# Reciprocal roots of the second layer's key-head sums by Newton steps on VectorE, and another order of that layer's weight units

## The chip, the cores and the metric

The kernel runs on one core of a Trainium2 chip. TensorE (PE in the profile) multiplies matrices, VectorE (DVE) and ScalarE (ACT) work element by element, GpSimd (POOL) does small things and starts the accumulating DMAs, SyncE (SP) starts the other DMAs. The engines have a queue each, which they work through in order; semaphores tie them together. The metric is the device time of one execution in microseconds, with the median over some executions.

## The reference

Two decoder layers on 512 tokens of width 1024, in float32. Each layer normalises, makes one wide projection, feeds four head groups from it, gates each group, and projects back onto the residual stream:

```python
h = rmsnorm(x, norm_g)
p = h @ W_in                        # 3488 columns, cut up among the groups
# A: latent attention (MLA), 4 heads, key = 64 plain + 32 rotary columns
# B: short gated convolution   C: chunked causal gMLP   D: MoBA, 4 heads, blocks of 256 keys
y = concat(A * silu(ga), B * silu(gb), C * silu(gc), D * silu(gd))
x = x + y @ W_out

def rmsnorm(x, g):
    y = x * lax.rsqrt(jnp.mean(x * x, axis=-1, keepdims=True) + EPS)
    return y * g
```

Queries and keys of the head groups are normalised per head as well. For four heads and 512 tokens, the sums of one kind (rs_q, rs_k for MLA, rs_mq, rs_mk for MoBA) fill a tile of 128 partitions x 16: four token tiles by four heads. The reciprocal root of such a tile is what is changed here.

## The kernel before, in words

A float32 product is made of three matmuls: each operand is split in a high part (rounded, whi, hTh, yTh) and a low part (the rest, wlo, hTl, yTl), and high x high, low x high and high x low are summed in PSUM. A weight unit (up to 128 x 1024) is loaded by SP into one of two raw buffers (NRAW), then `split_units` makes the high part by a copy on ACT or DVE, and `low_half` the low part by a subtraction on DVE, which frees the raw buffer for a later load.

In the second layer, the products are formed with sums of token parts and of weights. Units named p11 ... p22 and e11 ... e22 belong to the two big products so formed, ga, gb, gd and cb are the columns of gates and of the convolution; each has parts 0 and 1, which are units of their own. The unit names are cut in the profile: raw_p, whi_p, wlo_p for p.., px, py, pz for their results in PSUM, ex, ey, ez for those of e... Sums of weights are made by DMA: SP copies one operand, and then a DMA of POOL adds the other (t and in_w_o_dram in the rows).

No engine's order is written by hand. While the program is built, a planner (`Order`, `Chain`, `Slots`) keeps a clock for every engine and a cost for every instruction, and emits each instruction when its time has come. `main` walks the units in the order of a list, for the second layer `SEQ1`, and issues their matmuls whenever nothing of higher priority is due; the heads, norms and splits are chains that run beside it. So a change of the list or of one rule of splitting moves instructions on all engines, also far from the place. FAR is such a rule: a unit at least FAR units ahead of the one that PE is at is split in one instruction of 1024 columns instead of two of 512, if its index is over a bound.

The keys K of the second layer go through: squares and sums on ACT and DVE (`head_means`), eps added on DVE and the power on POOL (`head_rstd`, tile rs_k), two multiplications of K by rs_k on DVE (`key_scale`, 128x512 each), then transposes on PE (t1a; t0a is the same for Q), whose copies hi1a, lo1a, hi0a, lo0a enter the scores sa. The scores of head after head follow, first those of MLA (sa, pa, pTa, oa), and then those of MoBA (mq0d, mq1d, mk0d, mk1d, sd, pd, pTd, od), with products of units between them. zz is the high part of an operand of a later e product, yD what MoBA gives to the output projection (oz, ox, oy).

In the rows L190 is the helper that emits on ACT, DVE and POOL, L220 the one for PE and L384 the one for DMA.

Of the kernel before, what the change touches and what calls it, by code (L numbers as in the profile page):

```python
# [13 lines left out]
I32 = mybir.dt.int32  # L14
AF = mybir.ActivationFunctionType
ALU = mybir.AluOpType
AX = mybir.AxisListType

P = 128
S = 512  # L20
NT = S // P
D = 1024
# [27 lines left out]
EFEAT = ((2, 6), (10, 12))  # L50
TSE = 26000.0
SSUMS = {"p3": 0, "p2": 1, "p1": 2, "p22": 3}
SEQ1 = ['p11', 'p21', 'p3', 'p4', 'ga0', 'p2', 'p1', 'p22', 'ga1', 'e11', 'e21', 'e3', 'e4', 'e2', 'e1', 'cb0', 'e22', 'gb0', 'gd0', 'cb1', 'gb1', 'gd1']
K0, K1, KK = (2, 3, 0, 1), (4, 5, 6, 7), (0, 2, 3, 1)
ZPROD = ("b11", "t3", "b21", "t4", "t2", "t1", "b22")
TS0 = 58000.0
FAR = 3
DLO = ()
LZ = (True, False)
MLAGO = 'p4'  # L60
TZ1 = 270000.0
DLAND = 6000.0
SGLOAD = 'p3'
TAIL = ((0, 256), (256, 512))
# [106 lines left out]
def free_size(ap):  # L171
    n = 1
    for d in ap.shape[1:]:
        n *= d
    return n


class Chain:
# [26 lines left out]
        return self._emit("G", 290 + 2.0 * free_size(a[0]), f, a, k)  # L205

    def pow(self, f, *a, **k):
        return self._emit("G", 400 + 165 * free_size(a[0]), f, a, k)

    def pe(self, cost, f, *a, **k):  # L210
        if self.t != self.pe_t:
# [21 lines left out]
def hybrid_trunk(ctx: ExitStack, tc: tile.TileContext, x, positions, norm_g, w_c, w_f, w_t, w_o, mla_q_norm_g,  # L233
# [3 lines left out]
    V, A, G, PE = nc.vector, nc.scalar, nc.gpsimd, nc.tensor  # L237
# [16 lines left out]
    o = Order()  # L254
# [5 lines left out]
    t2S = Slots(o, NT2, lambda name, dt=F32: t2p.tile([P, S], dt, tag="t2", name=name))  # L260
# [43 lines left out]
    def dma(ch, nbytes, dst, src):  # L304

        o.clk["D"] = max(o.clk["D"], ch.t) + nbytes / 360.0
        move(nc.sync, dst, src)
        ch.t = o.clk["D"] + 2000.0

    x1d = dr.tile([S, D], F32, name="x1d")  # L310

# [36 lines left out]
    def add_unit(*a):  # L348
        u = Unit(*a)
        units[u.name] = u  # L350
        u.idx = len(order)
        order.append(u)
# [28 lines left out]
    def move(q, dst, src, **k):  # L381

        if len(src.shape) < 4:
            q.dma_start(dst, src, **k)  # L384
            return
        for g in range(2):
            q.dma_start(dst[:, 2 * g:2 * g + 2], src[:, g], **k)
# [11 lines left out]
    def t_sums(*streams):  # L399

        gap = 4000.0 if len(streams) == 1 else 3000.0
        for i in range(3):
            steps = []
            for l, src, t, b in streams:
                for n, x, y in (((f"{t}1", f"{b}11", f"{b}12"), (f"{t}3", f"{b}12", f"{b}22")),
                                ((f"{t}2", f"{t}1", f"{b}22"),), ((f"{t}4", f"{t}2", f"{b}21"),))[i]:
                    steps += [(l, src, n, x, y, j) for j in range(2)]
            for l, src, n, x, _, j in steps:
                o.clk["D"] = max(o.clk["D"], o.now) + 1500.0
                move(nc.sync, src(l, n, j), src(l, x, j))  # L410
                yield o.now + gap
            yield o.now + gap
            for l, src, n, _, y, j in steps:
                o.clk["G"] = max(o.clk["G"], o.now) + 1000.0
                move(nc.gpsimd, src(l, n, j), src(l, y, j), accum_op=ALU.add, max_dma_last_dim=1024)
                o.set(tsum_ev[l, n, j], o.now + 10000.0)
                yield o.now + gap
            yield o.now + (8000.0 if len(streams) == 1 else 0.0)
# [6 lines left out]
    for l in range(DEPTH):  # L425
# [3 lines left out]
        add_unit(mla_w_ukv[l], 1, 512, f"ukv_{l}")  # L429
        for n in SEQ1 if l in STOK else SEQ:  # L430
            if n in SPROD:
# [57 lines left out]
    def split_units(i0, i1):  # L489
        for u in order[i0:i1]:  # L490
            ch = Chain(o)
            if u.name != "c0_0":
                yield from ch.wait(u.loaded)
            u.hi, u.lo = yield from u.slots.get(ch, u.name)
            if u.name[:-2] in DLO:
                yield from dma_split(u, ch)
                continue
            n = u.a * u.b
            gain = {"uq": 2 * int(u.name[-1]), "ukv": 4 + int(u.name[-1])}.get(u.name[:-2])
            if gain is not None:  # L500
                yield from ch.wait(pc_ev)
            whole = False
            for i in range(2):
                if whole:
                    break
                if u.name == "c0_0":
                    yield from ch.wait(u.landed[i])
                while ch.t > o.now + SLACK:
                    yield ch.t - SLACK
                while not u.wanted and max(o.clk["A"], o.clk["V"]) > o.now + WSLACK:  # L510
                    yield o.now + 100.0
                whole = i == 0 and gain is None and u.idx >= at[0] + FAR and u.idx > 5
                c2 = Chain(o, max(o.now, ch.t))
                hi, lo, raw = (z[:, :n] if whole else u.part(z, i) for z in (u.hi, u.lo, u.raw))
                g = None
                if gain is not None:
                    c = gain + (i if u.a == 2 else 0)
                    g = pcol[:, c:c + 1]
                if o.clk["V"] + 900.0 < o.clk["A"] and u.idx > 3 or u.idx == 0 and i == 0:
                    if g is None:  # L520
                        yield from c2.dve_fast(V.tensor_copy, hi, raw)
                    else:
                        yield from c2.dve(V.tensor_scalar, hi, raw, g, None, op0=ALU.mult)
                else:
                    yield from c2.act(A.activation, hi, raw, AF.Copy, scale=1.0 if g is None else g)
                for j in range(2) if whole else (i,):
                    o.set(u.high[j], c2.t)
                o.spawn(low_half(u, i, c2, lo, raw, hi, g, whole), None, LOPRIO if u.idx < 4 else 5)
                ch.t = max(ch.t, c2.t - LAT)

    def dma_split(u, ch):

        while ch.t > o.now + SLACK:
            yield ch.t - SLACK
        while not u.wanted and max(o.clk["A"], o.clk["V"]) > o.now + WSLACK:
            yield o.now + 100.0
        ch.t = max(ch.t, o.now)
        yield from ch.act(A.activation, u.hi, u.raw, AF.Copy)
        for e in u.high:
            o.set(e, ch.t)  # L540
        yield from ch.act(A.activation, u.lo, u.hi.bitcast(F32), AF.Copy, scale=-1.0)
        u.raw_slots.put(ch)

        def add():
            while ch.t > o.now:
                yield ch.t
            o.clk["G"] = max(o.clk["G"], o.now) + 1000.0
            move(nc.gpsimd, four(u.lo) if u.name[:-3] in EPROD else u.lo, u.src, accum_op=ALU.add, max_dma_last_dim=1024)
            for e in (*u.half, u.ready):
                o.set(e, o.now + DLAND)  # L550
        o.spawn(add(), None, 4)

    def low_half(u, i, ch, lo, raw, hi, g, whole):
        while o.clk["V"] > o.now + VSLACK and u.idx > at[0] + URGENT:
            yield o.now + 100.0
        ch.t = max(ch.t, o.now)
        if g is None:
            yield from ch.dve(V.tensor_tensor, lo, raw, hi.bitcast(F32), op=ALU.subtract)
        else:
            yield from ch.dve(V.scalar_tensor_tensor, lo, in0=raw, scalar=g, in1=hi.bitcast(F32),  # L560
                              op0=ALU.mult, op1=ALU.subtract)
        o.set(u.half[i], ch.t)
        if whole:
            o.set(u.half[1], ch.t)
        if u.half[1 - i].t is not None:
            ch.t = max(ch.t, u.half[1 - i].t)
            u.raw_slots.put(ch)
            o.set(u.ready, ch.t)
# [10 lines left out]
    at = [0]  # L579
# [12 lines left out]
    nhalf = cst.tile([P, 4], F32, name="nhalf")  # L592
# [167 lines left out]
    for l in range(DEPTH):  # L760
        L = Layer()
# [255 lines left out]
    def head_means(ch, L, n, t, z):  # L1017
# [11 lines left out]
        yield from ch.dve(V.tensor_reduce, L.rs[n][:, t, :], sq, axis=AX.X, op=ALU.add)  # L1029
        t2S.put(ch)  # L1030

    def head_rstd(ch, L, n, eps):

        r = L.rs[n]
        if isinstance(eps, float):
            yield from ch.dve(V.tensor_scalar, r, r, 1.0, eps, op0=ALU.mult, op1=ALU.add)
        else:
            yield from ch.dve(V.tensor_tensor, r, r, eps.unsqueeze(2).to_broadcast([P, NT, 4]), op=ALU.add)
        r2 = r.rearrange("p t h -> p (t h)")
        yield from ch.pow(G.tensor_tensor, r2, r2, nhalf[:, 0:1].to_broadcast([P, 4 * NT]), op=ALU.pow)  # L1040
        o.set(L.rs_ev[n], ch.t)

    def key_scale(ch, L, n, K):
# [100 lines left out]
    def kv_chain(L, t, kv_ps, t0):  # L1144
# [25 lines left out]
        for i in range(NT):  # L1170
            yield from ch.wait(L.stat[i])
        yield from head_rstd(ch, L, "k", L.e2[:, :, 1])
        yield from key_scale(ch, L, "k", K[:, :, :, 0:64])
        o.set(L.kd, ch.t)
# [712 lines left out]
    def main():  # L1887
# [223 lines left out]
        for L in layers:  # L2111
# [21 lines left out]
            st, st2 = ({"bank": {}, "ev": {}, "f32": {}} for _ in range(2))  # L2133
            for n in SEQ1 if L.stok else SEQ:
                if n in EPROD:
# [133 lines left out]
    for l in STOK:  # L2269
        o.spawn(t_sums((l, z_src, "t", "b")), TZ1, 4)  # L2270
    o.spawn(start())
# [51 lines left out]
```

## Time and profile before

| what | value |
|---|---|
| median of 3 runs | 504.42 us (503.38 to 504.62) |
| profiled execution | 502.23 us, its span 500.5 us |
| mean granted clock of TensorE | 0.992 |
| PE busy | 480.7 us, 96% of the span |
| DVE, ACT, POOL busy | 398.2, 343.8, 137.1 us (80%, 69%, 27%) |

The first layer lasts until about 250 us, the second from there to the end. The span is the profiled time from the first to the last instruction; 1.7 us of the execution lie around it. Idle time of an engine stands in the rows in brackets, with the engine and tile that ended it. An engine that is busy 96% of the span sets the time except in its gaps.

### The profile page before, as it was taken

The numbers are of one execution on the slowest core, as the hardware profiler recorded it, in microseconds if no ns is written. First come the engines' busy times: TensorE is split into PE (matmuls) and PEld (weight loads), VectorE is DVE, ScalarE is ACT, GpSimd is POOL, SyncE is SP. The second block draws the span as 40 slices with busy tenths as digits, with TensorE's granted clock in tenths as the row PEclk, the third lists the DMA queues.
The fourth block names the chain that finished last, engine by engine and source line by source line (L and its number), as shares of the span: only waits on it lengthen the run. The fifth ranks groups of instructions, "written<-read, shape, count | busy, mean of one in ns | idle before, by whom it ended". The sixth has DMA issues, their size and how long they took to land.

```text
span 500.5 us, 7430 instructions
## 1 busy us (share of the span) xinstructions
PE 480.7 (96%) x2416; PEld 406.8 (81%) x2416; DVE 398.2 (80%) x781; ACT 343.8 (69%) x891; POOL 137.1 (27%) x201
## 2 busy tenths in 40 slices
PE   8999999999989999999999995999999979999996
PEld 7888888888878888888899874887888768888875
DVE  4697686677897887789896687797997789988982
ACT  5897856786457874365676888498985657986540
POOL 8839583601521052000120139060302200000000
PEclk9999999999999999999999999899999989999999
DMA  8856889999599697875762368683755844675762
GB/s 272 282 152 213 187 233 316 258 239 273 125 342 225 216 282 174 309 288 181 230 204 79 126 229 272 151 169 126 185 151 207 177 144 174 203 230 173 294 208 85
DMA packets 50271, 104.95 MB, mean 210 GB/s; under 512 B 6118, under 2 KB 31032, under 8 KB 49784
## 3 DMA queue, kind: packets, MB, share of 16 engines
q1 hardware_dynamic: 32656, 87.30, 50.3%
q0 software_dynamic: 17472, 17.10, 22.3%
q8 instruction: 19, 0.31, 0.2%
q14 instruction: 20, 0.16, 0.1%
q10 hardware_dynamic: 104, 0.07, 0.1%
HBM read 96.33 MB, written 41.68 MB: 276 GB/s over the span
## 4 chain that ended last, share of the span: by engine, by line
PE 78%; DMA 7%; DVE 5%; ACT 4%; issue 2%; POOL 2%; SPq 1%; DVEq 0%; POOLq 0%; ACTq 0%
PE oy L220 6%; PE kv L220 5%; PE cq L220 5%; PE oz L220 4%; PE sq L220 4%; PE ox L220 4%; PE ga L220 4%; PE gb L220 4%; PE gd L220 4%; PE cb L220 4%; PE py L220 3%; PE sa L220 3%; PE ez L220 2%; PE ex L220 2%; PE gc L220 2%
## 5 line engine op out<-in xcount | busy, mean ns | idle before, releaser
L190 ACT ACTIVATE pd<-pd,mnd 128x512 f32<-128x512 f32 (+3 forms) x58 | 30.6, 558 | 5.3 <-DVE mnd L190 5.2
L190 ACT ACTIVATE pa<-pa,mna 128x512 f32<-128x512 f32 (+3 forms) x56 | 29.2, 553 | 2.3 <-DVE mna L190 2.0
L384 POOL DMA_DIRECT2D t<-in_w_o_dram x16 | 20.3, 1346 | 28.6 <-DMA t<-t 27.9
L190 ACT ACTIVATE phd<-pTd 128x512 fp32r<-128x512 f32 (+1 forms) x24 | 12.6, 524 | 14.1 <-PE pTd L220 13.9
L190 ACT ACTIVATE whi_t<-raw_t 128x1024 fp32r<-128x1024 f32 x16 | 16.7, 1051 | 7.4 <-DMA raw_t<-t 7.3
L220 PE MATMUL cq<-whi_c,hTh 128*128 128x416 f32 x64 | 20.7, 368 | 0.8 <-ACT hTh L190 0.7
L190 ACT ACTIVATE pha<-pTa 128x512 fp32r<-128x512 f32 (+1 forms) x24 | 12.6, 527 | 12.6 <-PE pTa L220 12.5
L220 PE MATMUL cq<-whi_c,hTl 128*128 128x416 f32 x64 | 19.8, 356 | 1.0 <-DVE hTl L190 1.0
L190 DVE CUSTOM_DVE_ANT_0 pd<-sd,maskb,rs_mq 128x512 f32<-128x512 f32 (+3 forms) x32 | 16.7, 546 | 4.5 <-PE pTd L220 3.0
L220 PE MATMUL cq<-wlo_c,hTh 128*128 128x416 f32 x64 | 20.0, 358 | 0.0
L190 DVE CUSTOM_DVE_ANT_0 pa<-sa,maskb,rs_q 128x512 f32<-128x512 f32 (+3 forms) x32 | 16.4, 542 | 3.5 <-ACT junk L190 2.6
L190 DVE TENSOR_TENSOR wlo_t<-raw_t,whi_t 128x1024 fp32r<-128x1024 f32 x16 | 19.1, 1214 | 0.0
L190 DVE TENSOR_TENSOR wlo_p<-raw_p,whi_p 128x1024 fp32r<-128x1024 f32 (+1 forms) x18 | 18.1, 1016 | 0.0
L190 DVE TENSOR_TENSOR wlo_e<-raw_e,whi_e 128x512 fp32r<-128x512 f32 (+1 forms) x19 | 17.7, 936 | 0.3 <-ACT whi_e L190 0.2
L190 DVE TENSOR_TENSOR pla<-pTa,pha 128x512 fp32r<-128x512 f32 (+1 forms) x24 | 14.3, 596 | 4.2 <-ACT pha L190 4.1
L190 POOL TENSOR_SCALAR xss<-xss 128x1 f32<-128x1 f32 x4 | 2.5, 633 | 54.4 <-ACT jk L190 48.4
L190 ACT ACTIVATE whi_p<-raw_p 128x1024 fp32r<-128x1024 f32 (+1 forms) x14 | 11.9, 870 | 7.7 <-PE ga L220 4.0
L190 ACT ACTIVATE whi_e<-raw_e 128x512 fp32r<-128x512 f32 (+1 forms) x16 | 12.7, 812 | 5.2 <-DMA raw_e<-in_w_f_dram 4.7
L190 ACT ACTIVATE whi_b<-raw_b 128x1024 fp32r<-128x1024 f32 x12 | 12.6, 1056 | 5.3 <-DMA raw_b<-in_w_o_dram 5.2
L190 POOL TENSOR_TENSOR ms<-ms,nhalf 128x2 f32<-128x2 f32 x8 | 7.5, 943 | 31.4 <-DVE ms L190 23.4
L190 DVE TENSOR_TENSOR pld<-pTd,phd 128x512 fp32r<-128x512 f32 (+1 forms) x24 | 14.0, 596 | 2.3 <-ACT phd L190 2.2
L220 PE MATMUL pTd<-ident,pd 128*128 128x128 f32 x80 | 12.7, 273 | 3.2 <-ACT zz L190 3.1
(546 smaller groups left out, 1882.2 us busy)
## 6 DMA issues: line engine op xcount, KB each, us to landing
t<-in_w_o_dram POOLq DMA_DIRECT2D x16, 512.0 KB, 9.8
raw_t<-t SPq DMA_DIRECT2D x16, 512.0 KB, 4.5
raw_b<-in_w_o_dram SPq DMA_DIRECT2D x12, 512.0 KB, 4.5
t<-in_w_o_dram SPq DMA_DIRECT2D x8, 512.0 KB, 5.8
p<-in_w_t_dram POOLq DMA_DIRECT2D x8, 512.0 KB, 14.9
t<-t SPq DMA_DIRECT2D x8, 512.0 KB, 4.9
raw_p<-p SPq DMA_DIRECT2D x8, 512.0 KB, 4.1
raw_e<-e SPq DMA_DIRECT2D x8, 512.0 KB, 3.3
```

The lines of the kernel that those rows point to most:

```text
L190: f(*a, **k)
L220: f(*a, **k)
L384: q.dma_start(dst, src, **k)
```

## The change

The reciprocal root of rs_k in the second layer (only this one of the eight) is made by a first guess from the float's bits and three Newton steps: ten DVE instructions on 128x16, in a work tile named newton, where one power on POOL stood. In `SEQ1`, p2 stands ahead of ga0, ga1 ahead of p22, and gd0 behind cb1. FAR is 2 instead of 3, and the bound on the index is 10 instead of 5; this rule holds for both layers. POWC and DLAT are names for numbers that were there before, with the same values.

```diff
-SEQ1 = ['p11', 'p21', 'p3', 'p4', 'ga0', 'p2', 'p1', 'p22', 'ga1', 'e11', 'e21', 'e3', 'e4', 'e2', 'e1', 'cb0', 'e22', 'gb0', 'gd0', 'cb1', 'gb1', 'gd1']
+SEQ1 = ['p11', 'p21', 'p3', 'p4', 'p2', 'ga0', 'p1', 'ga1', 'p22', 'e11', 'e21', 'e3', 'e4', 'e2', 'e1', 'cb0', 'e22', 'gb0', 'cb1', 'gd0', 'gb1', 'gd1']
...
-FAR = 3
+FAR = 2
...
+NEWT = ("k",)
+POWC = 165
+DLAT = 2000.0
...
-                whole = i == 0 and gain is None and u.idx >= at[0] + FAR and u.idx > 5
+                whole = i == 0 and gain is None and u.idx >= at[0] + FAR and u.idx > 10
...
+    def newton_rstd(ch, r):
+
+        m = free_size(r)
+        tab = yield from t2S.get(ch, "newton")
+        y, z = tab[:, :m], tab[:, m:2 * m]
+        yield from ch.dve(V.tensor_scalar, y.bitcast(I32), r.bitcast(I32), -0.5, 1597463007.0, op0=ALU.mult, op1=ALU.add)
+        for i in range(3):
+            yield from ch.dve(V.tensor_tensor, z, y, y, op=ALU.mult)
+            yield from ch.dve(V.scalar_tensor_tensor, z, in0=z, scalar=-0.5, in1=r, op0=ALU.mult, op1=ALU.mult)
+            yield from ch.dve(V.scalar_tensor_tensor, r if i == 2 else y, in0=z, scalar=1.5, in1=y, op0=ALU.add, op1=ALU.mult)
+        t2S.put(ch)
+
     def head_rstd(ch, L, n, eps):
...
-        yield from ch.pow(G.tensor_tensor, r2, r2, nhalf[:, 0:1].to_broadcast([P, 4 * NT]), op=ALU.pow)
+        if L.l == 1 and n in NEWT:
+            yield from newton_rstd(ch, r2)
+        else:
+            yield from ch.pow(G.tensor_tensor, r2, r2, nhalf[:, 0:1].to_broadcast([P, 4 * NT]), op=ALU.pow)
         o.set(L.rs_ev[n], ch.t)
```

What this does to the engines' rows can only be seen in the program that the planner gives. PE has the same 2236 rows, DVE 792 instead of 775, ACT 614 instead of 636, POOL 166 instead of 169; the order changes in both layers.

On PE in the second layer, the transposes of Q and K for the first two MLA heads (t0a, t1a) before the change, nine matmuls of ga behind the last matmul of px:

```order
L220 MATMUL ga_1_3468<-hTh_1_2820,whi_ga_1_3341 128x512
L220 MATMUL ga_1_3468<-hTl_1_2821,whi_ga_1_3341 128x512
L220 MATMUL ga_1_3468<-hTh_1_2820,wlo_ga_1_3342 128x512
L220 MATMUL t0a_3482<-ident,Q_3032 96x128 x4
L220 MATMUL t1a_3483<-ident,K_3033 96x128 x4
L220 MATMUL ga_1_3468<-hTh_1_2820,whi_ga_1_3341 128x512
```

And now:

```order
L223 MATMUL py_1_3501<-whi_p_1_3459,yTh 128x512
L223 MATMUL py_1_3501<-wlo_p_1_3460,yTh 128x512
L223 MATMUL py_1_3501<-whi_p_1_3459,yTl 128x512
L223 MATMUL t0a_3618<-ident,Q_3040 96x128 x4
L223 MATMUL t1a_3619<-ident,K_3041 96x128 x4
L223 MATMUL py_1_3501<-whi_p_1_3488,yTh 128x512
```

They have moved 57 matmuls back: between px and t0a stand now 24 of py (unit p2), 24 of ga0 and 18 of py (unit p1). Behind t1a come 6 more of p1, 24 of ga1 and 6 of p22 ahead of the next scores sa.

On DVE, from the addition of eps to rs_k to the second multiplication of K; before:

```order
L190 TENSOR_TENSOR rs_k<-rs_k,e_2355 128x16
L190 TENSOR_TENSOR rbq_3364<-Q_3032,sinT 128x16x16
L190 TENSOR_TENSOR wlo_ga_1_3342<-raw_ga_1_3293,whi_ga_1_3341 128x1024
L190 TENSOR_TENSOR Q_3032<-Q_3032,cosT 128x16x32
L190 TENSOR_TENSOR yTl<-a_2931,yTh 128x4x128
L190 TENSOR_TENSOR yTl<-a_3013,yTh 128x4x128
L190 TENSOR_TENSOR Q_3032<-Q_3032,rbq_3364 128x16x32
L190 TENSOR_TENSOR wlo_p_1_3397<-raw_p_1_3352,whi_p_1_3396 128x1024
L190 TENSOR_TENSOR K_3033<-K_3033,rs_k 128x8x64
```

Now the first rows of the same stretch:

```order
L193 TENSOR_TENSOR rs_k<-rs_k,e_2345 128x16
L193 TENSOR_TENSOR rbq_3387<-Q_3040,sinT 128x16x16
L193 TENSOR_SCALAR newton<-rs_k 128x16
L193 TENSOR_TENSOR newton<-newton 128x16
L193 TENSOR_TENSOR rbq_3387<-Q_3040,sinT 128x16x16
L193 TENSOR_TENSOR wlo_p_1_3343<-raw_p_1_3299,whi_p_1_3342 128x1024
L193 SCALAR_TENSOR_TENSOR newton<-newton,rs_k 128x16
L193 TENSOR_TENSOR Q_3040<-Q_3040,cosT 128x16x32
```

The ten steps stand one by one among the other work, the last of them in row 495 (the eps is row 460), and the two multiplications of K in rows 499 and 506; before they were 8 and 12 rows behind the eps.

On ACT, where the MoBA heads of the second layer begin (mq1d and mk0d are operands of the first scores sd, whi_e and whi_cb the high parts of units of e and of cb0); before:

```order
L190 ACTIVATE mq0d_4289<-tmqd_4274 64x512
L190 ACTIVATE mk0d_4299<-tmkd_4275,pcol 64x512
L190 ACTIVATE whi_e_1_4277<-raw_e_1_4246 128x1024
L190 ACTIVATE mq1d_4302<-tmqd_4274 64x512
L190 ACTIVATE mk0d_4299<-tmkd_4275,pcol 64x512
```

And now:

```order
L193 ACTIVATE mq0d_4350<-tmqd_4344 64x512
L193 ACTIVATE mk0d_4360<-tmkd_4345,pcol 64x512
L193 ACTIVATE whi_cb_1_4311<-raw_cb_1_4306 128x1024
L193 ACTIVATE whi_e_1_4366<-raw_e_1_4309 128x1024
L193 ACTIVATE mq1d_4364<-tmqd_4344 64x512
L193 ACTIVATE mk0d_4360<-tmkd_4345,pcol 64x512
```

The whi_e in the new rows is that of unit e22 (part 0), which stood before behind the exponentials pd of the first MoBA head, directly ahead of the copy zz. On POOL, the first of the two accumulating DMAs that follow stands now ahead of a memset of kl1d, which waited for the first heads; before, both stood behind it.

More of the change, by code (lines that the diff above doesn't have):

```diff
@@ L207, in pow @@
     def pow(self, f, *a, **k):
-        return self._emit("G", 400 + 165 * free_size(a[0]), f, a, k)
+        return self._emit("G", 400 + POWC * free_size(a[0]), f, a, k)
     def pe(self, cost, f, *a, **k):
@@ L307, in dma @@
         move(nc.sync, dst, src)
-        ch.t = o.clk["D"] + 2000.0
+        ch.t = o.clk["D"] + (DLAT if o.now > 40000.0 else 2000.0)
     x1d = dr.tile([S, D], F32, name="x1d")
```

## The prediction

> **What bounds the kernel now.** I read the page's first two parts, then the waits of TensorE (PE), then the timelines of PE, GpSimd (POOL) and VectorE (DVE) round the largest wait, and last the windows, for the clock. First the page's busy shares:
>
> ```profile
> PE 480.7 (96%) x2416; PEld 406.8 (81%) x2416; DVE 398.2 (80%) x781; ACT 343.8 (69%) x891; POOL 137.1 (27%) x201
> ```
>
> PE is busy for 96% of the span, so only two things can change the time: a gap in PE's row of work, and a stretch in which PE works at a lower clock. The gaps of PE, as engine, line, what was waited for, and us in total, times, longest:
>
> ```profile
> PE t1a L220 <- DVE K L190: 5.4, 2, 3.5
> PE pTd L220 <- ACT zz L190: 3.1, 1, 3.1
> PE sd L220 <- DVE mq1d L190: 1.7, 1, 1.7
> ...
> PE cq L220 <- DVE hTl L190: 1.0, 1, 1.0
> PE px L220 <- ACT x L190: 0.8, 1, 0.8
> ```
>
> The largest is the one beside which the change is made: the transposes t1a of the second layer's MLA keys K wait for K. PE's own row there (start, us, what, and in brackets the idle time and its releaser):
>
> ```profile
> 304.04 0.39 PE L220 MATMUL px<-whi_p,hTl 128*128 128x512 f32 x1
> ...
> 306.31 0.60 PE L220 MATMUL t0a<-ident,Q 128*96 128x128 f32 x4
> 308.81 0.42 PE L220 MATMUL t1a<-ident,K 128*96 128x128 f32 x2 [1.90 <-DVE K L190]
> 312.72 0.66 PE L220 MATMUL t1a<-ident,K 128*96 128x128 f32 x2 [3.48 <-DVE K L190]
> ...
> 313.60 0.63 PE L220 MATMUL ga<-hTl,whi_ga 128*128 128x512 f32 x1
> ...
> 315.31 0.45 PE L220 MATMUL ga<-hTh,wlo_ga 128*128 128x512 f32 x1
> ...
> 324.47 0.40 PE L220 MATMUL sa<-hi1a,hi0a 96*128 96x512 f32 x1
> ```
>
> The two waits make 1.90 + 3.48 = 5.38 us. The cause stands one engine further, on POOL and then on DVE:
>
> ```profile
> 295.80 2.90 POOL L190 TENSOR_TENSOR rs_q<-rs_q,nhalf 128x16 f32<-128x16 f32 x1 [1.68 <-DVE rs_q L190]
> ...
> 300.35 7.69 POOL L190 TENSOR_TENSOR rs_k<-rs_k,nhalf 128x16 f32<-128x16 f32 x1 [0.96 <-DVE rs_k L190]
> ```
> ```profile
> 295.55 0.17 DVE L190 TENSOR_TENSOR rs_q<-rs_q,e 128x16 f32<-128x16 f32 x1 [2.10 <-ACT junk L190]
> ...
> 300.10 0.17 DVE L190 TENSOR_TENSOR rs_k<-rs_k,e 128x16 f32<-128x16 f32 x1
> 300.18 0.42 DVE L190 TENSOR_TENSOR rbq<-Q,sinT 128x256 f32<-128x256 f32 x1
> 300.51 1.22 DVE L190 TENSOR_TENSOR wlo_ga<-raw_ga,whi_ga 128x1024 fp32r<-128x1024 f32 x1
> 301.65 0.68 DVE L190 TENSOR_TENSOR Q<-Q,cosT 128x512 f32<-128x512 f32 x1
> ...
> 303.46 0.68 DVE L190 TENSOR_TENSOR Q<-Q,rbq 128x512 f32<-128x512 f32 x1
> 304.06 1.22 DVE L190 TENSOR_TENSOR wlo_p<-raw_p,whi_p 128x1024 fp32r<-128x1024 f32 x1
> 308.06 0.69 DVE L190 TENSOR_TENSOR K<-K,rs_k 128x512 f32<-128x512 f32 x1 [2.79 <-POOL rs_k L190]
> ```
>
> The power on rs_k (the reciprocal roots of the key heads' sums) lasts 7.69 us, the same shape on rs_q just before 2.90. The answer by tile gives its two uses, one in each layer (min, median, max in ns):
>
> ```profile
> L190 POOL TENSOR_TENSOR rs_k<-rs_k,nhalf x2: 2910/5298/7686, 62.6 to 300.3; 128x16 f32<-128x16 f32 x2
> ```
>
> In the first layer it took 2.91. DVE ran through its queue, reached K at 305.3 and stood for 2.79 us. With a power of 2.90 us it would have been done at 303.25 and nothing would have waited. The clock after the wait (stretch; busy us of PE, PEld, DVE, ACT, POOL; granted clock; DMA share; GB/s):
>
> ```profile
> 142.00:144.00 2.00, 1.42 (x8) 1.28 (x9) 1.94 (x4) 1.85 (x3) 0.96 (x1) 1.00 1.32 421
> 144.00:146.00 2.00, 2.00 (x10) 1.65 (x9) 1.94 (x6) 1.52 (x4) 0.00 (x0) 1.00 0.88 289
> ...
> 312.00:314.00 2.00, 1.28 (x4) 1.11 (x5) 2.00 (x5) 1.60 (x4) 0.00 (x0) 0.50 1.17 185
> 314.00:316.00 2.00, 2.00 (x7) 1.58 (x6) 2.00 (x3) 0.00 (x0) 0.00 (x0) 0.65 1.16 177
> ...
> 404.00:406.00 2.00, 2.00 (x7) 1.58 (x6) 2.00 (x6) 1.86 (x4) 0.00 (x0) 0.54 0.46 53
> 406.00:408.00 2.00, 2.00 (x7) 1.55 (x6) 2.00 (x5) 0.78 (x2) 0.00 (x0) 0.61 0.83 288
> ```
>
> After the K wait it is 0.50 and 0.65, after the zz wait (3.11 us, near 400) 0.54 and 0.61; after the wait of 1.7 us (sd, near 143) it stays 1.00. At 313.60 to 315.31 five matmuls come 0.43 apart; undisturbed, the chain of waits has 30 in 6.80 us, 0.227 each:
>
> ```profile
> 317.83 6.80 PE py L220 x30
> ```
>
> So the low clock costs about 6 × 0.20 = 1.2 us at each of the two places.
>
> The Trainium skill ("TensorE: Matmul & The Clock Gate", Part 1 with the section on HAM oscillation) says that only idle gaps above about 3.4 us throttle the array again. The gap of 3.48 agrees; the one of 3.11 does not, unless the 0.3 us is uncertainty of the records. By the page a new wait up to 3.4 us would leave the 1.2 us gained; by the rows it might not. The sum goes by the rows.
>
> **The change part by part.** *Power to Newton.* Ten DVE instructions on 128x16 take the place of one power. A 128x16 row lasts 0.17 us and the next one starts after 0.08 (300.10 to 300.18), so they hold DVE for 10 × 0.08 to 10 × 0.17, that is 0.8 to 1.7 us, on an engine that is 80% busy. On POOL 7.69 us go; what stood behind it (two powers of the value norms) starts sooner, and nobody on PE waited for those.
>
> *Where they stand.* They are not issued back to back. Between the addition of eps (row 460 of the new DVE order) and the second K (row 506) I count 6 instructions of 128x1024 (300.51 to 301.65: 1.14 each), 17 of 128x512 (303.46 to 304.06: 0.60 each), 4 products and 5 fused ones of 128x256 (0.33 and about 0.40 each), 2 statistics of about 0.35 (estimated between these), and 12 of 128x16 and less (0.09 each). The sum is 6.8 + 10.2 + 1.3 + 2.0 + 0.7 + 1.1 = 22.1 us. Between the eps of rs_q and that of rs_k there now stand one 1024, one 512 and two 256: 1.14 + 0.60 + 0.80 + 0.1 = 2.6 us instead of 4.55. With rs_q's eps at 295.55 as now, that of rs_k comes at 298.2 and K is done at 298.2 + 22.1 = 320.3. The ends are an eps at 300.10 as now (322.2) and one as early as rs_q's (317.7).
>
> *When PE comes for it.* t1a stood 9 matmuls behind the last px and now stands 66 behind (24 py, 24 ga, 18 py). The last px starts at 304.04 and ends its slot at 304.27; the px wait of 0.8 us goes, since ScalarE (ACT) has fewer splits ahead of that copy. PE is at t0a at 303.5 + 66 × 0.227 = 318.5, at t1a at about 318.9. The wait that is left is 320.3 − 318.9 = 1.4 us, between 0 and 3.3. A wait of 1.4 is nearest to the row of 1.7, after which the clock held. Local sum: 5.4 + 1.2 + 0.8 − 1.4 = 6.0 us gained, between 2.9 (3.3 left and the clock lost again) and 7.4.
>
> *What comes later for it.* The first scores sa started at 324.47. Now 36 matmuls (8.2 us) and the four t1a (0.3) stand between: 318.9 + 1.4 + 8.5 = 328.8, 4.3 us later, while the second layer's attention must end at the same place in PE's row. Its last link and its taker:
>
> ```profile
> 464.75 0.62 ACT L190 ACTIVATE yD<-yad 128x512 fp32r<-128x512 f32 x1
> ```
> ```profile
> 465.91 0.68 DVE L190 TENSOR_TENSOR yD<-yad,yD 128x512 fp32r<-128x512 f32 x1
> ```
> ```profile
> 469.23 0.39 PE L220 MATMUL oz<-whi_b,yD 128*128 128x512 f32 x1
> ```
>
> The low part of yD is done at 466.6, 2.6 us ahead of its matmul. To keep 6.0 us, the row of attention heads must become 4.3 + 6.0 − 2.6 = 7.7 us shorter. What can shorten it is that 10.9 us of product matmuls (48 of 0.227) now lie ahead of sa and no longer between the heads, and their splits with them. PE and DVE are what the heads share with that work:
>
> ```profile
> 325.00:350.00 25.00, 24.02 (x131) 20.31 (x130) 22.02 (x53) 21.73 (x73) 8.82 (x6) 1.00 0.60 148
> 350.00:375.00 25.00, 25.00 (x139) 21.65 (x140) 23.76 (x56) 22.63 (x67) 4.96 (x3) 1.00 0.64 164
> ```
>
> PE has 98% and DVE 92% there, so most of 10.9 is freed, not all. I take a shortening of 6.2, between 0 and 10.9: 1.5 us lost at the end, between 0 and 6.0 (all of the gain).
>
> *Start of the MoBA heads.* Today this stretch loses the zz wait and the clock behind it, 3.1 + 1.2 = 4.3 us:
>
> ```profile
> 401.81 0.63 ACT L190 ACTIVATE whi_e<-raw_e 128x512 fp32r<-128x512 f32 x1 [4.65 <-DMA raw_e<-in_w_f_dram]
> ...
> 402.77 0.60 ACT L190 ACTIVATE zz<-zT 128x512 f32<-128x512 f32 x1
> ```
> ```profile
> 390.67 2.11 POOL L384 DMA_DIRECT2D t<-in_w_o_dram  x2
> ```
> ```profile
> 392.83 8.96 DMA raw_e<-in_w_f_dram
> ```
>
> A weight load (raw_e, unit e22), issued just behind two accumulating DMAs of POOL, takes 8.96 us; ACT stands 4.65 us at its split with zz behind it. In the new order the split of e22 is one 1024 wide instruction and stands on ACT ahead of mq1d and of the second mk0d, which the first MoBA scores need; zz no longer has it in front. So one stall is exchanged for another on the same load. I take no net change, between +4.3 (both vanish) and −5.9 (ACT held for all 8.96 plus 1.2 of clock, against 4.3).
>
> *First layer.* FAR and the index bound reorder the splits there too, and by 22 fewer ACT instructions over the kernel. The cq wait of 1.0 may go, since one split stands behind hTl instead of ahead; the sd wait of 1.7 comes from a load that holds ACT, and in the new order another load holds it nearby. Taken as 0, between +2.7 (both waits gone) and −2.0 (estimate: one more wait like the sd one).
>
> **Sum.** 6.0 − 1.5 + 0 + 0 = 4.5 us. The profiled execution took 502.23 us, 500.5 of it the span; it becomes 497.7. The median of the runs, 504.42, is 2.2 above that execution: 504.4 − 4.5 = 499.9, say 500. For the faster/same/slower chances I use 0.3%, about 1.5 us, which is about what a measurement of this kernel tells from no change.
>
> **Rivals.** *The heads give it back.* If DVE, at 92%, and not PE sets the pace of the heads, the shortening is near 0, yD comes 4.3 us later than now and past its 2.6 us of slack, PE waits there, and the gain of 6.0 is gone: 504 to 506, by the rows 504.4 + 4.3 − 2.6 = 506.1 at worst. For it: DVE at 23.76 of 25. Against it: PE has no idle time there at all, and much of that DVE work is splits that have moved.
>
> *The stretched power is of one execution only.* Three other executions of the same kernel would then have no K wait, and only the 0.8 us would be gained: 503.6. For it: the same power took 2.91 in the first layer and 2.90 on rs_q. Against: those runs are slower than the profiled one, not faster.
>
> *Newton does nothing, the order does all.* A power of 7.69 from 298.3 would end at 306, and K is wanted at 318.9. So the place of t1a alone cures the wait, and the ten instructions, spread over DVE's queue, even delay K. This gives the same 500 and only moves the credit.
>
> *Slower: the e22 load in front of the first MoBA scores.* The mechanism is the one above: ACT in order, mq1d behind a split whose load runs against the accumulating DMAs. It costs the difference between ACT's hold and what PE has in front; from a new stall of 9 us on (4.5 more than today's 4.3) the gain is eaten. If the zz wait of 4.3 stays as well, since ACT's queue is late, the whole is 8.96 + 1.2 = 10.2 worse: 510. Between 4.65 (today's hold on that load, 504.6) and that I put it at 507. For it: the 8.96 us, and the first of the two accumulating DMAs is now ahead of a small memset that waits long. Against it: another load in the same place (raw_cb) is issued well before and the load now starts earlier too.
>
> *All goes well.* No wait left at t1a, MoBA's stall half gone, cq gone: 7.4 + 2.1 + 1.0 = 10.5, 494.
>
> **How the numbers follow.** Forecast (faster by 2 to 8, 496 to 502): 0.52, with Newton or the order as the cause. All well: 0.11, faster. Heads give it back: 0.13, of which 0.08 within 0.3% and 0.05 slower. One execution only: 0.08, within. Slower by e22: 0.16, of which 0.02 within. Faster 0.63, same 0.18, slower 0.19. The likeliest case's range is 496 to 502; for 8 in 10 it must reach into the rivals on the slow side, to 507, and may leave out the best tenth: 496 to 507.
>
> **What would show it.** Right: PE's wait t1a <- K below 2 us, a clock of 1.00 after it, no px wait; sa near 328 in the profile; K ready with rs_k from DVE, POOL without rs_k in the second layer. Wrong: a wait of oz or of later products for yD or the heads; ACT at whi_e for over 6 us with sd of the first MoBA head behind it; new waits before 250 us; or t1a waiting over 3 us with a clock of 0.5 behind it, which would say that K's place on DVE is too late.

## The result and the profile after

| | median | lowest to highest | executions |
|---|---|---|---|
| before | 502.12 us | 499.90 to 504.62 | 20 |
| changed | 499.93 us | 492.77 to 502.94 | 20 |

The ratio is 0.9895, with a 95% interval of 0.9866 to 0.9924; it is taken over executions within 1.5% of each kernel's fastest, which leaves out ten of the changed kernel's twenty, since they spread over 10 us, and none of before. Over all executions the quotient of the medians is 0.9956 and that of the means 0.9939 (499.15 by 502.21). So the change gains 2 to 5 us. The forecast was 500.0, in a range of 496 to 507, and faster. The profiled execution of the changed kernel took 502.94 us (span 501.2), the longest of its twenty, so it shows the gain and what spoils it side by side, and no gain in total.

PE's waits in the profile of the changed kernel (engine, line, what was waited for; us in total, times, longest):

```profile
PE pTd L223 <- DVE zz L193: 4.9, 1, 4.9
PE t1a L223 <- DVE K L193: 2.1, 1, 2.1
PE t1a L223 <- ACT mix L193: 1.6, 1, 1.6
PE pTd L223 <- ACT mk1d L193: 1.2, 1, 1.2
...
PE oz L223 <- DVE yD L193: 0.4, 1, 0.4
...
PE px L223 <- ACT x L193: 0.3, 1, 0.3
```

The K wait is 2.1 us instead of 5.4 and the px wait 0.3 instead of 0.8. The zz at the top is a new one: it lies in the first layer, near 190 us, and the 3.1 us of zz near 403, in the second layer, are gone. Two marks on PE's timeline part the time between the layers: the first transpose of the second layer's normalised input, and the last matmul. Before, and now:

```profile
247.25 0.60 PE L220 MATMUL hT<-ident,h 128*128 128x128 f32 x4
...
496.17 0.28 PE L220 MATMUL ot<-whi_b,yTl 128*128 128x256 f32 x1
```
```profile
253.54 0.60 PE L223 MATMUL hT<-ident,h 128*128 128x128 f32 x4
...
496.91 0.28 PE L223 MATMUL ot<-whi_b,yTl 128*128 128x256 f32 x1
```

From the first mark to the second it takes 248.92 us before and 243.37 now. **In these two executions the second layer is 5.5 us shorter, the first layer 6.3 us longer.** The experiments below show the same parting: every kernel with the old rule for splits in the first layer reaches the first mark at 246.1 to 248.4 us, every one with the new rule at 252.3 to 254.3.

The place of the change, on DVE and on PE of the changed kernel:

```profile
304.20 0.18 DVE L193 TENSOR_TENSOR rs_k<-rs_k,e 128x16 f32<-128x16 f32 x1 [0.57 <-ACT junk L193]
...
304.63 0.17 DVE L193 TENSOR_SCALAR newton<-rs_k 128x16 int32<-128x16 int32 x1
...
321.34 0.13 DVE L193 SCALAR_TENSOR_TENSOR rs_k<-newton 128x16 f32<-128x16 f32 x1
...
326.80 0.67 DVE L193 TENSOR_TENSOR K<-K,rs_k 128x512 f32<-128x512 f32 x1
```
```profile
324.63 0.60 PE L223 MATMUL t0a<-ident,Q 128*96 128x128 f32 x4
325.06 0.38 PE L223 MATMUL t1a<-ident,K 128*96 128x128 f32 x2
327.52 0.42 PE L223 MATMUL t1a<-ident,K 128*96 128x128 f32 x2 [2.08 <-DVE K L193]
```

Between the first Newton step and the last lie 16.7 us, though nine of the ten last 0.13 to 0.17 us (one 0.61): the rest is other DVE work between them. PE comes 20 us after eps, where it came 6 us after eps before, and so it waits little. In the window after this wait (columns as in the prediction: PE, PEld, DVE, ACT, POOL, clock, DMA share, GB/s) the clock stays whole:

```profile
328.00:332.00 4.00, 4.00 (x19) 3.30 (x18) 4.00 (x6) 3.90 (x15) 0.76 (x1) 1.00 1.16 166
```

It doesn't always. A second profile of the same kernel (after_again, an execution of 501.95 us) has the same wait at the same place, 2.07 us, and the clock falls to 0.63; PE gets 13 matmuls into the 4 us instead of 19:

```profile
327.92 0.42 PE L223 MATMUL t1a<-ident,K 128*96 128x128 f32 x2 [2.07 <-DVE K L193]
```
```profile
328.00:332.00 4.00, 4.00 (x13) 3.22 (x14) 4.00 (x7) 3.56 (x14) 1.15 (x2) 0.63 1.15 177
```

The first layer, in the changed kernel, as SyncE's queue, the chain of waits and DVE show it:

```profile
183.99 0.33 SPq L387 DMA_DIRECT2D raw_gc<-in_w_f_dram  x1
```
```profile
183.99 9.02 DMA raw_gc<-in_w_f_dram
```
```profile
182.72 1.20 DVE L193 TENSOR_TENSOR wlo_gb<-raw_gb,whi_gb 128x1024 fp32r<-128x1024 f32 x1
...
193.04 0.69 DVE L193 CAST whi_gc<-raw_gc 128x1024 fp32r<-128x1024 f32 x1 [6.71 <-DMA raw_gc<-in_w_f_dram]
...
194.26 0.69 DVE L193 SCALAR_TENSOR_TENSOR zz<-cc,chs 128x512 f32<-128x512 f32 x1
```

The same three before, from SyncE, ACT and DVE:

```profile
171.91 0.34 SPq L384 DMA_DIRECT2D raw_gc<-in_w_f_dram  x1
```
```profile
180.45 1.04 ACT L190 ACTIVATE whi_gc<-raw_gc 128x1024 fp32r<-128x1024 f32 x1
```
```profile
170.66 1.22 DVE L190 TENSOR_TENSOR wlo_gb<-raw_gb,whi_gb 128x1024 fp32r<-128x1024 f32 x1
...
186.50 0.69 DVE L190 SCALAR_TENSOR_TENSOR zz<-cc,chs 128x512 f32<-128x512 f32 x1
```

The low part wlo_gb, which frees a raw buffer, now comes at 182.72 instead of 170.66, and the load of raw_gc 12 us later with it. The split of that unit has moved from ACT to DVE, with one row (pld) between it and zz. DVE stands 6.71 us for the load, PE 4.91 us for zz (by the profile's naming; pld ends at the same moment, and both stand behind the split), and the clock falls behind it:

```profile
190.00:200.00 10.00, 5.61 (x22) 4.79 (x23) 5.82 (x11) 1.93 (x3) 1.99 (x3) 0.83 0.58 216
```

### The profile page after: what moved, and what is told of

The parts are those of the page before. It is cut to its first block, busy times and chain, and to the rows that moved or that the text cites. A ratio compares the mean times of both kernels' runs of the same rounds, so it can differ in the third digit from the quotient of the medians.

```text
span 501.2 us, 7407 instructions
## 1 busy us (share of the span) xinstructions
PE 481.0 (96%) x2416; PEld 405.9 (81%) x2416; DVE 403.6 (81%) x801; ACT 331.6 (66%) x853; POOL 127.6 (25%) x200
## 4 chain that ended last, share of the span: by engine, by line
PE 65%; DMA 14%; DVE 11%; ACT 5%; issue 2%; SPq 0%; POOL 0%; DVEq 0%; ACTq 0%
PE cq L223 7%; PE oy L223 6%; PE kv L223 5%; PE sq L223 4%; PE gb L223 4%; DMA raw_e<-in_w_f_dram 4%; PE cb L223 3%; PE sa L223 3%; PE ez L223 2%; PE su L223 2%; PE gc L223 2%; PE ga L223 2%; PE ox L223 2%; PE oz L223 2%; DMA raw_ch<-in_w_f_dram 2%
## 5 line engine op out<-in xcount | busy, mean ns | idle before, releaser
L193 ACT ACTIVATE pd<-pd,mnd 128x512 f32<-128x512 f32 (+3 forms) x54 | 28.8, 560 | 7.9 <-DVE mnd L193 7.7
L387 POOL DMA_DIRECT2D t<-in_w_o_dram x16 | 18.4, 1253 | 18.7 <-DMA t<-t 18.6
L223 PEld LDWEIGHTS pTd<-ident,pd 128*128 128x128 f32 x80 | 10.1, 141 | 11.8 <-DVE zz L193 5.3
L193 DVE TENSOR_TENSOR wlo_e<-raw_e,whi_e 128x1024 fp32r<-128x1024 f32 x14 | 16.8, 1211 | 3.2 <-ACT whi_e L193 3.2
L193 DVE CUSTOM_DVE_ANT_0 pd<-sd,maskb,rs_mq 128x512 f32<-128x512 f32 (+3 forms) x32 | 16.7, 545 | 1.8 <-PE pTd L223 1.0
L193 ACT ACTIVATE whi_b<-raw_b 128x1024 fp32r<-128x1024 f32 x11 | 11.5, 1057 | 9.7 <-PE gc L223 4.9
L193 POOL TENSOR_TENSOR rs_mq<-rs_mq,nhalf 128x16 f32<-128x16 f32 x2 | 5.9, 2930 | 46.6 <-ACT junk L193 33.2
L193 DVE TENSOR_TENSOR wlo_p<-raw_p,whi_p 128x1024 fp32r<-128x1024 f32 (+1 forms) x15 | 17.0, 1141 | 0.1
L387 POOL DMA_DIRECT2D p<-in_w_t_dram x8 | 9.6, 1698 | 26.6 <-DMA p<-p 24.4
L193 POOL TENSOR_TENSOR rs_mk<-rs_mk,nhalf 128x16 f32<-128x16 f32 x2 | 5.8, 2920 | 39.8 <-DVE rs_mk L193 39.8
## 6 DMA issues: line engine op xcount, KB each, us to landing
p<-in_w_t_dram POOLq DMA_DIRECT2D x8, 512.0 KB, 16.7
```

Of the source, the lines that this page charges most:

```text
L193: f(*a, **k)
L223: f(*a, **k)
```

## The experiments

Theories: A, the K wait is the gain; A1, by a faster root; A2, by the later place of t1a alone. B, the rules for order and splits bring it. C, what is gained at K is given back behind it. Each experiment is also measured by its two stretches, as above: the start of the second layer's first transpose, and from there to the last matmul. The stretches are those of one profiled execution each. Beside the experiments, before was run again, with medians of 501.69, 501.84 and 501.51 us; each ratio is to the one that ran beside it.

| kernel | ratio to before (95%) | median, us | first stretch | second stretch |
|---|---|---|---|---|
| before | | 502.1 | 247.25 | 248.92 |
| changed | 0.9895 (0.9866 to 0.9924) | 499.93 | 253.54 | 243.37 |
| changed, again | 0.9884 (0.9839 to 0.9929) | 499.59 | 253.88 | 242.02 |
| newton_only | 1.0246 (1.021 to 1.0281) | 514.07 | 248.35 | 257.29 |
| seq_only | 1.0279 (1.0252 to 1.0306) | 516.00 | 246.96 | 261.79 |
| far_only | 1.0227 (1.0189 to 1.0265) | 514.78 | 253.00 | 256.91 |
| no_newton | 1.0131 (1.0063 to 1.02) | 509.45 | 254.29 | 250.99 |
| no_seq | 1.0138 (1.0097 to 1.0178) | 510.45 | 252.29 | 252.16 |
| no_far | 1.0122 (1.0084 to 1.0159) | 507.60 | 247.31 | 254.36 |
| pow_late | 1.0098 (1.0065 to 1.013) | 506.15 | 246.56 | 251.51 |
| newton_in_place | 0.9961 (0.9934 to 0.9987) | 499.75 | 246.62 | 247.08 |
| power_in_place | 0.994 (0.9902 to 0.9977) | 499.80 | 252.27 | 241.42 |
| far_l1 | 0.9853 (0.9804 to 0.9903) | 493.83 | 246.58 | 240.45 |
| far_l1, again | 0.9818 (0.9771 to 0.9865) | 493.28 | 246.13 | 239.46 |

**Parts one by one.** newton_only keeps Newton and takes back the order and both numbers of the split rule:

```diff
-SEQ1 = ['p11', 'p21', 'p3', 'p4', 'p2', 'ga0', 'p1', 'ga1', 'p22', ...
+SEQ1 = ['p11', 'p21', 'p3', 'p4', 'ga0', 'p2', 'p1', 'p22', 'ga1', ...
-FAR = 2
+FAR = 3
-... u.idx >= at[0] + FAR and u.idx > 10
+... u.idx >= at[0] + FAR and u.idx > 5
```

> Before with the Newton steps alone (old unit order, old rule for whole splits). The first layer's order is that of before; in the second, t1a now stands 46 rows behind the last px instead of 10. Theory A (the K wait is the gain, and a late place of t1a or a fast root cures it): t1a <- K below 2 us instead of 5.4, clock 1.00 behind it, 4 to 6 us less than before, ratio about 0.990. Theory B (the whole-split rule and the unit order bring the gain): within 1.5 us of before, ratio 0.997 to 1.003.

It is 12 us slower than before, which neither theory forecast. The K wait fell to 2.5 us (theory A: below 2), and yet the second stretch is 8.4 us longer. The waits behind K:

```profile
PE t1a L223 <- DVE K L193: 2.5, 2, 1.8
PE sd L223 <- DVE yaa L193: 2.2, 1, 2.2
PE sd L223 <- DVE mnd L193: 1.8, 2, 1.4
PE oy L223 <- ACT sumh L193: 1.5, 1, 1.5
```

They lie all along the heads. More than the gain is given back here (theory C): the planner makes the whole order behind K anew, and this one is bad.

seq_only keeps the new unit order alone (NEWT empty, FAR and the index as before), far_only the split rule alone (NEWT empty, old SEQ1).

> Before with the new order of the second layer's units alone; the power stays on GpSimd and t1a stays 10 rows behind px. Theory A: the K wait stays as long as the power is stretched (about 5 us with a power of 7.7 us), ratio 0.997 to 1.003. If the power is 2.9 us here, its stretch belonged to the one execution, the wait is below 1 us and the time is about 5 us lower. Theory B: 3 to 5 us less than before, with the K wait still there.

> Before with the rule for whole splits alone (FAR 2, index over 10). The first layer's order is that of the changed kernel. Theory A: the K wait stays at 4 to 5 us (t1a 13 rows behind px); and if the late load of raw_gc, which holds VectorE ahead of zz, belongs to this order, a zz wait of up to 5 us with a low clock behind it appears near 190 us: 0 to 5 us more than before, ratio 1.000 to 1.010. Theory B: 3 to 5 us less.

Both are slower, by 2.8% and 2.3%, so B fails for either alone. In seq_only the K wait is 4.4 us, and the power is stretched as in the profile before. far_only shows the first stretch at 253.00, as the changed kernel does, so those 6 us belong to the split rule; which of its two numbers does it was not tried. Its K wait is 2.5 us, not the 4 to 5 expected, since the power isn't stretched. This is GpSimd in seq_only, and then in far_only:

```profile
300.06 7.68 POOL L193 TENSOR_TENSOR rs_k<-rs_k,nhalf 128x16 f32<-128x16 f32 x1 [0.96 <-DVE rs_k L193]
```
```profile
306.65 2.89 POOL L193 TENSOR_TENSOR rs_k<-rs_k,nhalf 128x16 f32<-128x16 f32 x1
```

So the long power was no accident of one execution, but it is bound to its place: where it starts 6 us later, it takes 2.89 us. The last section shows what VectorE does meanwhile.

pow_late leaves before as it is and only tells the planner a cost of 7.7 us for this power:

```diff
+        if L.l == 1 and n == "k":
+            yield from ch._emit("G", 7700.0, G.tensor_tensor, (r2, r2, ...), {"op": ALU.pow})
```

> Before, with the power kept on GpSimd, and only the planner's cost for the rs_k power of the second layer set to 7.7 us instead of 3.04. No arithmetic changes; t1a is now put 31 rows behind px instead of 10. Theory A in the form that the place of t1a alone is enough: the K wait falls below 1.5 us though the power is as slow as before, 4 to 6 us less, ratio about 0.990, like Newton alone. In the form that the power itself must go: the wait stays above 3 us and the time within 1.5 us of before.

The power takes 8.82 us here, the longest of all, and the K wait still falls to 2.4 us, between the two values that were forecast: the place alone takes away more than half of it, as A2 says. The time rises by 1%, by waits for c (2.7), th_ga (1.9), yaa (1.8) and pa (1.7) behind it. Again C, and again the order.

**Only the instruction, with the order held still.** The parts change the order each time, so two kernels exchange the root alone; every other row on every engine stands as it stood. newton_in_place is before with the ten steps, back to back, in place of the power (scratch in the free columns of junk):

```diff
-        yield from ch.pow(G.tensor_tensor, r2, r2, ...)
+        if L.l == 1 and n == "k":
+            yield from ch._emit("G", 400 + 165 * free_size(r2), newton_now, (r2,), {})
+        else:
+            yield from ch.pow(G.tensor_tensor, r2, r2, ...)
```

> Before, word for word in its order on every engine, except that the one power on rs_k in the second layer is replaced by ten Newton instructions on VectorE, back to back, in the same place; the planner isn't told. Theory A (the K wait is the cost and Newton cures it): eps at 300.1, ten steps of 0.09 to 0.17 us, K done at about 306.9 and 309.3; t1a <- K falls from 5.4 to about 2 us and the clock stays at 1.00, 4 to 5 us less than before, ratio 0.990 to 0.993. Theory C (what is gained at K is given back at the next late thing): the K wait falls as much, but the waits behind it (zz, c, lo1a) grow, ratio 0.996 to 1.003.

DVE of this kernel, and PE's two t1a:

```profile
299.87 0.18 DVE L1035 TENSOR_SCALAR junk<-rs_k 128x16 int32<-128x16 int32 x1
...
301.76 0.18 DVE L1039 SCALAR_TENSOR_TENSOR rs_k<-junk 128x16 f32<-128x16 f32 x1
...
306.98 0.68 DVE L190 TENSOR_TENSOR K<-K,rs_k 128x512 f32<-128x512 f32 x1
...
309.51 0.68 DVE L190 TENSOR_TENSOR K<-K,rs_k 128x512 f32<-128x512 f32 x1
```
```profile
307.80 0.40 PE L220 MATMUL t1a<-ident,K 128*96 128x128 f32 x2 [1.18 <-DVE K L190]
310.24 0.66 PE L220 MATMUL t1a<-ident,K 128*96 128x128 f32 x2 [2.04 <-DVE K L190]
```

Ten steps take 2.1 us, one every 0.21, each on the result of the one before; the power took 7.69. The wait falls by 2.2 us, from 5.4 to 3.2, and the second stretch by 1.8; the zz wait near 400 stays at 3.2. The ratio of 0.9961 lies at the edge of C's range, but the sign of C, longer waits behind K, is not there; A1 is right in kind and too large. So this is what the arithmetic alone is worth in the old order: 2 us (0.7 to 3.3 by the interval). It isn't more, because the K rows stand behind 5 us of other DVE work there, and behind the two waits the clock still falls:

```profile
308.00:312.00 4.00, 1.96 (x8) 1.46 (x7) 3.23 (x7) 2.44 (x4) 0.00 (x0) 0.69 1.04 384
```

power_in_place is the changed kernel with the power where the first Newton step stood, and nothing for the other nine.

> The changed kernel, word for word in its order on every engine, except that the ten Newton instructions are gone and one power on GpSimd stands where the first of them stood. If the order does all and Newton nothing: the power of 2.9 to 8.8 us ends by 315, K is wanted after 320, t1a <- K is at most what it was (2.1 us) and about 1 us less since ten rows left VectorE; ratio to before 0.986 to 0.990. If Newton itself brings the gain: the K wait is 4 us or more, ratio 0.997 or above.

```profile
305.93 2.89 POOL L1045 TENSOR_TENSOR rs_k<-rs_k,nhalf 128x16 f32<-128x16 f32 x1
```

It takes 499.80 us, the changed kernel 499.93 and 499.59; the means over all executions are 498.93 against 499.15 and 498.45. The ratio of 0.994 lies in neither of the two forecast ranges, but its interval overlaps that of the changed kernel, and no execution of this run is left out of it, where ten are of the changed kernel's. The K wait is 2.3 us, the second stretch 241.42 against 243.37 and 242.02. **In the new order Newton's arithmetic is worth nothing that can be measured.** The power ends at 308.8, more than 15 us before K is wanted.

**Pairs of parts.** no_far is the changed kernel without the split rule, no_newton with the power at the planner's own cost, no_seq with the old unit order.

> The changed kernel without the new rule for whole splits: Newton and the unit order, first layer as in before. t1a stands 100 rows behind px. If parts add up from the single ones (1.025 and 1.028): 1.03 to 1.05. If the gain needs the unit order and Newton together and the rule for splits only costs: 0.985 to 0.995. If all three are needed: 1.01 to 1.03, with several waits of 1 to 3 us after 330 us.

> The changed kernel with the power again and the planner's own cost for it, so that the order is made anew: t1a is 13 rows behind px. The run with the power in place has told whether Newton's arithmetic matters; this one tells whether the order that it brings about does. If it does: as the single parts, 1.01 to 1.03. If unit order and split rule are enough: 0.985 to 0.995, with a K wait of 2 to 5 us.

> The changed kernel with the old order of units: Newton and the split rule. t1a is 34 rows behind px. If all three parts are needed: 1.01 to 1.03, several waits of 1 to 3 us after 330 us and the first layer as in the changed kernel. If Newton and the split rule are enough: 0.985 to 0.995.

All three are slower than before by 1.2 to 1.4%: taking back any one part of the change costs 8 to 11 us, and any one alone costs 12 to 14. Nothing adds up. no_newton and power_in_place have the same arithmetic and differ by the order that the planner made (splits included): 509.45 against 499.80. Newton's role in the change is that the planner, which sees ten steps in a full queue, puts t1a and all behind it elsewhere.

**The first layer taken back.** far_l1 is the changed kernel with the old split rule for the first layer:

```diff
-                whole = i == 0 and gain is None and u.idx >= at[0] + FAR and u.idx > 10
+                whole = i == 0 and gain is None and (u.idx >= at[0] + 2 if u.name.endswith("_1") else u.idx >= at[0] + 3 and u.idx > 5)
```

> The changed kernel with the new rule for whole splits in the second layer alone; the first layer keeps the order of before. If the zz wait near 190 us (4.9 us and 1.5 of clock in the profiled run) comes from the first layer's new order, it is gone; the first layer then ends about 5 us sooner than in the changed kernel's profile. If the second layer keeps what it has: 493 to 497 us, ratio 0.982 to 0.990. If its order, which the planner makes anew, loses as the single parts did: 500 to 512, ratio 0.998 to 1.02.

Its waits on PE, in the profile of the first of its two runs:

```profile
PE sd L223 <- ACT mk0d L193: 1.9, 1, 1.9
PE t1a L223 <- DVE K L193: 1.6, 1, 1.6
PE sd L223 <- DVE mq1d L193: 1.4, 1, 1.4
```

No wait above 2 us is left. The zz wait near 190 is gone, since raw_gc is loaded at 171.49 again and split on ACT (at 180.03):

```profile
171.49 0.33 SPq L387 DMA_DIRECT2D raw_gc<-in_w_f_dram  x1
```

To compare it with the changed kernel on one chip, both were run once more.

> The changed kernel again, for its time beside far_l1 on one chip and a second profile. Its twenty executions lay between 492.8 and 502.9. If the zz wait near 190 us is the cause of the spread (a load of raw_gc whose landing varies), the wait here is smaller than 4.9 us by about as much as the execution is below 502.9; the second layer loses 13 to 15 us as before. Ratio 0.986 to 0.992.

> far_l1 again, beside the changed kernel on one chip. If the first layer's order is worth what the two profiles say (18.3 us lost there against 12.0, of which the profile of a slow execution may overstate some): 3 to 6 us below the changed kernel, ratio to before 0.980 to 0.988. If it was the chip or chance: equal to the changed kernel within 1.5 us.

far_l1 takes 493.28 us beside 499.59: 6.3 us less, and about 8 us less than before. Its first stretch is 7.0 and 7.8 us shorter than the changed kernel's in the two pairs of profiles, its second 2.9 and 2.6 us: the planner made the second layer's order anew as well, so not all of the gain need be the first layer's. In the changed kernel the zz wait is 3.6 us this time and DVE's hold at raw_gc 5.4, against 4.9 and 6.7, but the first stretch is no shorter (253.88): the clock behind the wait is lower, 0.56 and 0.58 from 192 to 196 and to 200 us, against 0.74 and 0.84. That this load sets the spread of the times is not shown. The executions of far_l1 lie between 492.52 and 499.36 in the first run and between 491.61 and 495.12 in the second.

## Why the prediction was right, step by step

The total was right (500.0 against 499.9), its direction too, but that it agrees so closely is luck. The 4.5 us were taken off 504.42, the median of three executions; that of twenty is 502.12, and 502.1 − 4.5 would have given 497.6. The medians differ by 2.2 us, the means by 3.1. Of the four terms of the sum one failed and one was mis-sized, with opposite signs. As the profiles show them, the terms are 5.0 − 2.1 + 3.0 − 6.3 = −0.4 us: the profiled execution, forecast at 497.7, took 502.94, and the executions that do gain, down to 492.77, have no profile.

- *The K wait* (6.0 gained, 2.9 to 7.4). Right in the path and nearly in size: 1.4 us of wait were forecast to be left, 2.1 were. From eps to the second K it took 304.20 to 327.47, 23.3 us against 22.1 counted, and rs_k's eps came 3.3 us behind rs_q's instead of 2.6, since DVE waited 0.57 us for a square sum of ACT. Gained are 5.4 − 2.1 of wait, 0.5 of px and 1.2 of clock, 5.0; in the second profile the clock fell, and 3.8 are left. One reading was wrong: I wrote that with a power of 2.90 us nothing would have waited. In newton_in_place the root is done at 301.94, earlier than that, and t1a still waits 3.2 us.
- *The heads* (1.5 lost). Of the mechanism in the form forecast, yD late, 0.4 us is to be seen, so the size came out near (2.1 lost) for another reason. Other waits of this row came in its place: pla 0.9, less the 0.8 of lo1a that went, and t1a of the next heads stood 1.6 us for mix, as ACT was held 4.65 us by a load that took 11.15 (in the second profile ACT is held there for 1.77 us, and neither mix nor pla costs PE over 0.2):

```profile
340.68 1.06 ACT L193 ACTIVATE whi_e<-raw_e 128x1024 fp32r<-128x1024 f32 x1 [4.65 <-DMA raw_e<-in_w_f_dram]
341.64 0.46 ACT L193 ACTIVATE mix<-mp,sgb 128x256 f32<-128x256 f32 x1
```

- *Start of the MoBA heads* (taken as 0). Mis-sized by some 3 us: I expected the e22 load to hold ACT ahead of mq1d as it held zz. It held it for 0.51 us only, and sd waited 0.5; the 3.1 of zz, the 1.2 of clock behind it and 0.4 of c were gained, and a wait of 1.2 for mk is new:

```profile
396.56 1.06 ACT L193 ACTIVATE whi_e<-raw_e 128x1024 fp32r<-128x1024 f32 x1 [0.51 <-DMA raw_e<-in_w_f_dram]
```

- *First layer* (taken as 0, down to −2.0). This step failed; new waits before 250 us were one of the prediction's own signs of being wrong. It measured −6.3 in one profile and −6.6 in the other, against the bound of one more wait of 1.7. I had looked at the start and at the sd wait, which did go; I had not followed on each queue what stands ahead of zz there. The order shows it: in the new one the split of raw_gc stands on DVE two rows ahead of zz. The kind of wait was known, a load in front of the heads, and I had priced it in the second layer only.

Of the rivals, "the order does all" was given no chance of its own, and it is what the runs show. "One execution only" is refuted by seq_only and pow_late. "The heads give it back" did not befall the whole, but waits of that kind stand in the parts and pairs: yaa 2.2 in newton_only, yad 3.1 in far_only and no_seq, yD 3.4 in no_newton. "Slower by e22" did not come.

The Trainium skill ("TensorE: Matmul & The Clock Gate", HAM oscillation) gives as its rule that PE should have no idle gap above about 3.4 us. The runs show the clock fall behind shorter gaps too. A wait of 2.29 us in power_in_place was followed by the first of these rows, one of 2.66 in pow_late by the second:

```profile
327.00:331.00 4.00, 4.00 (x12) 3.17 (x11) 3.62 (x5) 3.90 (x15) 0.71 (x1) 0.57 1.18 180
```
```profile
395.00:399.00 4.00, 4.00 (x18) 3.27 (x19) 3.94 (x8) 3.39 (x8) 0.00 (x0) 1.00 0.61 210
```

So neither the page's 3.4 us nor my line between 1.7 and 3.1 decides it; the same length goes either way, at t1a of the changed kernel even the same wait. What decides it stays open.

## What to carry to other kernels

Where a planner orders the program, a changed instruction is also a changed cost, and the cost may move everything behind it. To learn what the instruction itself is worth, exchange it with the order held still, and read the rest as a change of order; parts of such a change do not add up, and the whole has to be measured. And where a rule of the planner holds for several stages, look at each stage by itself: here one stage gained 5.5 us, another lost 6.3, and keeping the rule out of the stage that lost gave 8 us in place of 2. And a forecast that starts from the median of three executions carries their error: here 2.3 us, more than the gain by the medians.

## What the runs showed of the hardware that was not expected

- The same GpSimd power on 128x16 takes 2.89 to 2.96 us in most places, 3.2 to 4.4 in some, and 7.69, 7.68 and 8.82 near 300 us in before, seq_only and pow_late. No run varied the cause alone, but the rows point at VectorE. In the three long cases VectorE goes through TENSOR_TENSORs without a gap from before the power's start. That run ends at 305.28, 304.99 and 305.72 us, and the power 2.76, 2.75 and 2.75 us later, about its usual length. In pow_late:

```profile
299.65 8.82 POOL L190 TENSOR_TENSOR rs_k<-rs_k,nhalf 128x16 f32<-128x16 f32 x1 [0.96 <-DVE rs_k L190]
```
```profile
303.37 2.35 DVE L190 TENSOR_TENSOR wlo_p<-raw_p,whi_p 128x1024 fp32r<-128x1024 f32 x2
308.36 0.69 DVE L190 CAST whi_p<-raw_p 128x1024 fp32r<-128x1024 f32 x1 [2.64 <-DMA raw_p<-p]
```

A shorter stretch ends in the same way: in seq_only wlo_e ends at 353.39, and the power on rs_mq, of 3.77 us, at 356.18. In far_only VectorE stands idle as the power starts at 306.65; it takes 2.89, and the TENSOR_TENSORs that come later run beside it at their usual length. So the long power looks like a wait for a break in VectorE's row, and K, which stands behind that row, must then wait for the power.
- Ten dependent instructions on 128x16 follow each other on VectorE every 0.21 us. With other work between them, in the changed kernel, the next row starts 0.06 to 0.09 us after eight of them, 0.20 after one with a dependent one behind it, and 0.54 after one.
- The granted clock fell to 0.57 behind a wait of 2.29 us and stayed at 1.00 behind others of 2.08, 2.46 (far_only) and 2.66. The wait of t1a, 2.08 and 2.07 us in two executions of the changed kernel, left it at 1.00 in one and at 0.63 in the other.
